# Second projections of two squared-ReLU MLPs: seven products of quarters in place of eight, sums kept on chip, and other buffer counts

## The chip, the cores and the metric

The kernel runs on one core of a Trainium2 chip. The metric is the time of one execution on the device in microseconds (us), the median of the runs that were made. Each run's profile also gives a span, which is the time from its first to its last recorded instruction.

## What is computed

Two transformer blocks follow each other on 512 tokens of width 1024, in float32. The first block has a hybrid mixer, a cross attention and a gated MLP. The second block has two layers, and each of them has a mixer (a sparse attention in the first, a gated linear attention in the second), a layer norm, an MLP and another layer norm. The change touches only the two MLPs of the second block. What one of them computes, cut from the reference:

```python
def sqrelu_mlp(x, w1, w2):
    return jnp.square(jax.nn.relu(x @ w1)) @ w2
...
        x = layer_norm(ALPHA * x + mix, ln1_g[i], ln1_b[i])
        x = layer_norm(ALPHA * x + sqrelu_mlp(x, mlp_w1[i], mlp_w2[i]), ln2_g[i], ln2_b[i])
```

Here x is 512 x 1024, w1 is 1024 x 4096 and w2 is 4096 x 1024. So the second projection multiplies a 512 x 4096 hidden matrix by w2 and adds the result to ALPHA times x.

## The kernel before, in words

**Precision.** Every float32 matrix is held as two parts, a rounded high part and the rest, the low part (class `Split`). One product of two such matrices is three matmuls in one PSUM group: high by high, high by low, low by high (`mm`). A weight piece of 128 x 512 is made into its parts by one ScalarE copy (high) and one VectorE subtraction (low), in `split`. In the profile the parts are the tiles wh and wl, and wr is the raw tile that the DMA fills.

**The MLP (`mlp`).** The 4096 hidden units are taken in eight rounds of 512. In a round, four calls of `proj_t` compute four hidden tiles of 128 hidden units by 512 tokens: 8 products of 128 x 128 by 128 x 512, so 24 matmuls each, with weights from `unit_t` (one raw tile of 512 KB, split in two halves). ScalarE takes the ReLU out of PSUM into the tile r, VectorE or GpSimd squares it (`either`), and ScalarE and VectorE split it into the pair hid. Then `proj_n` of the round before runs: four weight units (`unit_n`), and for each of 4 token tiles and 2 halves of the 1024 output columns a PSUM group of 4 x 3 = 12 matmuls of 512 columns. Each group is added into x by one VectorE instruction (round 0 multiplies x by ALPHA in the same instruction). The last round's projection is returned as steps and runs together with the layer norm that follows (`tail`, `ln_norm`), whose output is transposed for the next stage.

**Buffers.** Four pools matter. Raw tiles wr come from a pool of `N_RAW` = 3. Pages of 1056 float32 (`N_PAGE` = 33) hold the two parts of a weight unit (two pages), of a hidden pair (one page) and of the transposed input (eight pages). Half pages of 512 (`N_HALF` = 18) hold r and similar tiles. PSUM has eight banks.

**Order.** The program is first recorded (`Recorder`), and a planner (`Plan`) sets the order of every engine's instructions by a list schedule over its own prices. So first projections of one round and second projections of the one before can be interleaved. A load may start only when its raw tile is free and when the unit nine places ahead of it in the list `units` has been used for the last time (the quota, 9 in the MLPs). A tile may take a buffer ahead of older ones only within the limits of `rules`: two PSUM banks and two pages are kept back for older tiles, and at most ten older PSUM tiles may be passed over. Where the plan shows TensorE idle for over 1 us, `emit` fills the gap with matmuls of the identity (`warm`), which show in the profile as `ps<-ident` 128x512.

All calls are issued from one place, so every row of the profile has line L509. The tile names tell the operations apart.

Of the kernel before, what the change touches and what calls it, by code (L numbers as in the profile page):

```python
# [7 lines left out]
F32 = mybir.dt.float32  # L8
F32R = mybir.dt.float32r
I32 = mybir.dt.int32  # L10
BF16 = mybir.dt.bfloat16
AF = mybir.ActivationFunctionType
OP = mybir.AluOpType
# [3 lines left out]
P = 128  # L17
# [6 lines left out]
ALPHA = 4.0 ** 0.25  # L24
# [3 lines left out]


PAGE = 1056  # L30
N_PAGE = 33
N_HALF = 18
N_RAW = 3
ROUNDS = 8
BIAS = 0.0

# [8 lines left out]
def is_ap(x):  # L45
    return hasattr(x, "ap") and hasattr(x, "tensor") and hasattr(x, "offset")


def on_chip(x):
    return type(x.tensor).__name__ == "Tile"  # L50
# [19 lines left out]
def region(ap):  # L70

    per = 1
    for s in list(ap.tensor.shape)[1:]:
        per *= int(s)
    dims = [(int(s), int(n)) for s, n in ap.ap]
    p0, f0 = divmod(int(ap.offset), per)
    pn = dims[0][1] if dims[0][0] else 1
    mask = 1
    for s, n in sorted((s, n) for s, n in dims[1:] if s and n > 1):
        m = 0  # L80
        if s == 1 and mask == 1:
            m = (1 << n) - 1
        else:
            for k in range(n):
                m |= mask << (k * s)
        mask = m
    return ap.tensor.name, p0, p0 + pn, mask << f0
# [10 lines left out]
class Recorder:  # L98
# [10 lines left out]
    def add(self, forms, bias=0.0):  # L109

        if self.held is not None:
            self.held += forms[0]
            return
        o = Op()
        o.i = len(self.ops)
        o.reads, o.writes, o.keep = [], [], self.keep
        for eng, method, args, kw in forms[0]:
            outs = [kw["out"] if "out" in kw else args[0]]
            if kw.get("accum_out") is not None:
                outs.append(kw["accum_out"])  # L120
            ins = [x for x in (args if "out" in kw else args[1:]) if is_ap(x)]
            ins += [x for k, x in kw.items() if k not in ("out", "accum_out") and is_ap(x)]
            for x in outs + ins:
                if on_chip(x):
                    self.tiles[x.tensor.name] = x.tensor
            o.writes += [region(x) for x in outs if on_chip(x)]
            o.reads += [region(x) for x in ins if on_chip(x)]
        o.forms = [(f[0][0], f) + price(f) + (bias if f[0][0] == "vector" else 0.0, port(f)) for f in forms]
        self.ops.append(o)
        return o  # L130
# [57 lines left out]
def port(calls):  # L188

    for eng, m, args, kw in calls:  # L190
        if eng not in ("vector", "gpsimd") or m in ("memset", "iota", "dma_start"):
            continue
        out = kw["out"] if "out" in kw else args[0]
        ins = [x for x in list(args[1:]) + [x for k, x in kw.items() if k not in ("out", "accum_out")] if is_ap(x)]
        room = [x for x in ins if "PSUM" not in str(x.space) and width(x) > 1]
        if eng == "gpsimd" or len(room) > 1:
            return True
        if m in ("tensor_copy", "tensor_scalar") and room and "PSUM" not in str(out.space):
            return True
    return False  # L200


def price(calls):

    t = sum(price1(*c) for c in calls)
    eng = calls[0][0]
    return t, {"tensor": 0.22, "scalar": 0.16, "vector": 0.12, "gpsimd": 0.12, "sync": 0.9}[eng]
# [325 lines left out]
class Block:  # L533
    def __init__(self, ctx, tc, a, out):
# [4 lines left out]
        self.const = E(tc.tile_pool(name="const", bufs=1))  # L539
        self.wp = E(tc.tile_pool(name="wp", bufs=N_RAW))  # L540
        self.pgp = E(tc.tile_pool(name="pgp", bufs=N_PAGE))
        self.s2p = E(tc.tile_pool(name="s2p", bufs=N_HALF))
# [257 lines left out]
    def proj_n_steps(self, part, w, r0, alpha=None, us=None, fine=False):  # L800
# [4 lines left out]
        for i in range(NT):  # L805
            for h in self.HALVES:
# [9 lines left out]
                        nc.vector.scalar_tensor_tensor(xv, xv, alpha, ps, op0=OP.mult, op1=OP.add)  # L816
                yield

    def setup(self):
        nc, a, cp = self.nc, self.a, self.const  # L820
        for i in range(NT):
            for c in self.HALVES:
                nc.sync.dma_start(self.x[:, i, c], a["x"][0, i * P:(i + 1) * P, c])
        self.identr = cp.tile([P, P], F32R, name="ident")
        self.ident = self.identr.bitcast(F32)
        t = self.s2()
        nc.gpsimd.memset(t[:, 0:P], 0.0)
        nc.gpsimd.affine_select(t[:, 0:P], t[:, 0:P], pattern=[[-1, P]], compare_op=OP.not_equal, fill=1.0, base=0,
                                channel_multiplier=1)
        nc.vector.tensor_copy(self.identr, t[:, 0:P])  # L830

        self.mnegr = cp.tile([P, P], F32R, name="mnegr")
        nc.gpsimd.memset(t[:, P:2 * P], 0.0)
        nc.gpsimd.affine_select(t[:, P:2 * P], t[:, P:2 * P], pattern=[[-1, P]], compare_op=OP.is_ge, fill=NEG, base=0,
                                channel_multiplier=1)
        nc.vector.tensor_copy(self.mnegr, t[:, P:2 * P])
        self.cols = {}
# [503 lines left out]
    def mlp(self, l, xT):  # L1341
        nc, a = self.nc, self.a
        w1, w2 = a["mlp_w1_2"][l], a["mlp_w2_2"][l]
        self.rules(9)
        self.early = 5
        prev = None
        for c in range(8):
            hid = []
            for j in range(4):
                ps = self.proj_t(self.unit_t(w1, (c * 4 + j) * P), xT)  # L1350
                r = self.s2("r")
                nc.scalar.activation(r, ps, AF.Relu)
                self.either("tensor_mul", r, r, r)
                h = self.pair("hid")
                self.split(h.hi, h.lo, r)
                hid.append(h)
            if prev:
                self.proj_n(prev, w2, (c - 1) * 512, None if c > 1 else ALPHA)
            prev = hid
        return self.proj_n_steps(prev, w2, 7 * 512, fine=l == 1)  # L1360

    def nsa(self, xT):
# [532 lines left out]
```

## Time and profile before

| what | value |
|---|---|
| median of 3 runs | 1964.53 us (1963.47 to 1973.55) |
| profiled execution, time | 1964.42 us |
| profiled execution, span | 1962.6 us |
| TensorE matmul busy | 1930.5 us (98%) |
| TensorE weight load busy | 1645.3 us (84%) |
| VectorE busy | 1214.9 us (62%) |
| ScalarE busy | 824.2 us (42%) |
| GpSimd busy | 78.5 us (4%) |
| mean granted TensorE clock | 0.994 |

PE is TensorE's matmuls, PEld its weight loads, DVE VectorE, ACT ScalarE, POOL GpSimd, SPq the queue that issues the DMAs. Matmuls are pipelined and overlap in the records, so the time that one takes in a stream is the distance between two starts, not its recorded length. The same holds for VectorE and ScalarE instructions that follow each other without a wait. The MLPs take roughly 1010 to 1376 us and 1590 to 1955 us of the span, each with parts of its neighbours at the ends.

### The profile page before, as it was taken

To read this page: it belongs to the slowest core of one execution; us is meant where nothing else is said; L and a number is where in the kernel's file an instruction comes from. 1 tells how busy PE (TensorE), PEld (TensorE's weight loads), DVE (VectorE), ACT (ScalarE), POOL (GpSimd) and SP (SyncE) were. 2 spreads that over 40 slices of the span, in tenths; PEclk is the share of its full clock that TensorE was granted. 3 is DMA by queue.
4 is the path that set the end of the run, shared out by engine and by line. 5 is a ranking of instruction groups with operands and counts; after the bars stand their busy time and mean duration, and the time that the engine had idled before them with its cause. 6 is when DMAs were issued, how large, how long until landed. Compare 5 with 4: busy or idle time off the path is not lost.

```text
span 1962.6 us, 26913 instructions
## 1 busy us (share of the span) xinstructions
PE 1930.5 (98%) x10348; PEld 1645.3 (84%) x10348; DVE 1214.9 (62%) x2690; ACT 824.2 (42%) x1673; POOL 78.5 (4%) x123
## 2 busy tenths in 40 slices
PE   9999999999999999999999999999999999999998
PEld 8888889798888878988788888778998988888776
DVE  5999665565434457688884345347686775344356
ACT  5476534344322333576534233233575434223330
POOL 0021000000000000012200000000000000000001
PEclk9999999999999999999999999999999999999999
DMA  6222423323222433510332233243223322233241
GB/s 172 80 69 65 155 87 103 97 65 118 65 76 75 118 108 83 110 32 22 99 106 76 75 108 97 75 127 104 76 76 97 98 76 91 67 98 105 70 150 43
DMA packets 215466, 177.38 MB, mean 90 GB/s; under 512 B 25174, under 2 KB 194202, under 8 KB 215338
## 3 DMA queue, kind: packets, MB, share of 16 engines
q1 hardware_dynamic: 215338, 175.66, 30.6%
q8 instruction: 81, 1.33, 0.3%
q14 instruction: 47, 0.39, 0.1%
HBM read 173.54 MB, written 2.10 MB: 89 GB/s over the span
## 4 chain that ended last, share of the span: by engine, by line
PE 86%; DVE 9%; ACT 3%; DMA 2%; issue 1%; SPq 0%; POOL 0%; DVEq 0%; ACTq 0%
PE ps L509 86%; DVE wl L509 2%; DVE sm L509 1%; DVE gcv L509 1%; ACT wh L509 1%; ACT p L509 1%; DMA wr<-in_mlp_w_dram 1%; DVE xtl L509 0%; DVE x L509 0%; DVE pt L509 0%; DMA wr<-in_w_up_dram 0%; ACT xth L509 0%; DMA g<-in_norm_mix_g_dram 0%; DMA wr<-in_w_down_dram 0%; DMA wr<-in_a_w_out_dram 0%
## 5 line engine op out<-in xcount | busy, mean ns | idle before, releaser
L509 ACT ACTIVATE wh<-wr 128x512 fp32r<-128x512 f32 x625 | 357.1, 623 | 423.5 <-PE ps L509 271.5
L509 DVE TENSOR_TENSOR wl<-wr,wh 128x512 fp32r<-128x512 f32 x625 | 406.2, 686 | 205.6 <-PE ps L509 96.8
L509 PE MATMUL ps<-xth,wh 128*128 128x512 f32 (+1 forms) x1464 | 516.9, 353 | 0.4 <-ACT hg L509 0.4
L509 PE MATMUL ps<-xtl,wh 128*128 128x512 f32 (+1 forms) x1464 | 514.4, 351 | 1.4 <-DVE xtl L509 1.4
L509 PE MATMUL ps<-xth,wl 128*128 128x512 f32 (+1 forms) x1464 | 513.4, 351 | 0.0
L509 PE MATMUL ps<-wh,hid 128*128 128x512 f32 (+1 forms) x1392 | 436.4, 391 | 1.8 <-ACT wh L509 1.7
L509 PEld LDWEIGHTS ps<-wh,hid 128*128 128x128 f32 x1392 | 260.3, 188 | 61.6 <-ACT wh L509 3.3
L509 PEld LDWEIGHTS ps<-xtl,wh 128*128 128x128 f32 x1464 | 276.2, 189 | 41.4 <-DVE xtl L509 2.6
L509 PEld LDWEIGHTS ps<-xth,wh 128*128 128x128 f32 x1464 | 276.4, 189 | 40.2 <-ACT xth L509 0.8
L509 PEld LDWEIGHTS ps<-xth,wl 128*128 128x128 f32 x1464 | 275.7, 188 | 39.9 <-DVE wl L509 0.2
L509 PE MATMUL ps<-wl,hid 128*128 128x512 f32 (+1 forms) x696 | 272.4, 391 | 1.6 <-DVE wl L509 1.5
L509 DVE TENSOR_TENSOR x<-x,ps 128x512 f32<-128x512 f32 (+1 forms) x210 | 141.1, 678 | 162.8 <-PE ps L509 162.2
L509 PEld LDWEIGHTS ps<-wl,hid 128*128 128x128 f32 x696 | 130.8, 188 | 34.2 <-DVE wl L509 4.8
L509 DVE TENSOR_TENSOR r<-r 128x512 f32<-128x512 f32 x62 | 42.8, 691 | 99.8 <-ACT r L509 99.7
L509 PE MATMUL ps<-wl,xth 128*128 128x256 f32 (+2 forms) x320 | 94.4, 295 | 3.4 <-DVE wl L509 3.4
L509 PE MATMUL ps<-wh,xth 128*128 128x256 f32 (+2 forms) x320 | 94.7, 296 | 0.0
L509 PE MATMUL ps<-wh,xtl 128*128 128x256 f32 (+2 forms) x320 | 93.9, 293 | 0.0
L509 ACT ACTIVATE r<-ps 128x512 f32<-128x512 f32 x64 | 38.0, 593 | 114.9 <-PE ps L509 114.9
L509 DVE SCALAR_TENSOR_TENSOR cv<-ps,cols,cv 128x511 f32<-128x511 f32 (+2 forms) x56 | 41.8, 746 | 39.1 <-ACT cv L509 38.5
L509 PEld LDWEIGHTS ps<-wl,xth 128*128 128x128 f32 x320 | 60.4, 189 | 5.6 <-DVE wl L509 4.2
L509 PE MATMUL ps<-wh,o 128*128 128x512 f32 x192 | 62.3, 394 | 0.0
L509 PEld LDWEIGHTS ps<-wh,xth 128*128 128x128 f32 x320 | 60.3, 189 | 1.4
(352 smaller groups left out, 2438.9 us busy)
## 6 DMA issues: line engine op xcount, KB each, us to landing
wr<-in_mlp_w_dram SPq DMA_DIRECT2D x128, 512.0 KB, 4.2
wr<-in_w_up_dram SPq DMA_DIRECT2D x44, 512.0 KB, 3.9
wr<-in_c_w_in_dram SPq DMA_DIRECT2D x24, 512.0 KB, 3.8
wr<-in_w_down_dram SPq DMA_DIRECT2D x22, 512.0 KB, 3.6
wr<-in_w_in_dram SPq DMA_DIRECT2D x16, 512.0 KB, 4.3
wr<-in_w_xkv_dram SPq DMA_DIRECT2D x16, 512.0 KB, 3.8
wr<-in_w_out_dram SPq DMA_DIRECT2D x8, 512.0 KB, 4.5
wr<-in_w_xq_dram SPq DMA_DIRECT2D x8, 512.0 KB
```

Source lines behind the costliest of these rows:

```text
L509: getattr(getattr(self.rec.nc, eng), method)(*args, **kw)
```

## The change

The second projection of rounds 0 to 6 of each MLP is done by the Winograd form of Strassen's scheme. The hidden tiles are taken two at a time (K of 256), and each pair is cut into quarters of 128 hidden units by 256 tokens. The 256 rows of w2 that belong to it are cut into quarters of 128 rows by 512 columns. Seven products of such quarters take the place of eight.

- `quad` makes the left sides from a pair of squared tiles: four additions or subtractions of 256 columns, and splits of one quarter of 256 columns and three tiles of 512 columns. It fills three pages and one half page, where the two hidden pairs took two pages.
- `wquad` loads two raw tiles (the 256 rows of w2) and makes the seven right sides when they are asked for. Four of the seven need a subtraction of 512 columns first, written over a quarter of the raw tile. Each right side is split into a page of its own. So both raw tiles stay taken until the last product (`p4`) has been made.
- `proj_s` takes the place of `proj_n` in rounds 0 to 6: for each product and each of two token tiles a PSUM group of 2 x 3 = 6 matmuls of 512 columns. Three of the products are added into x, four are kept as sums in half pages over all seven rounds (eight tiles; the first round copies them out with ScalarE).
- `join` adds the eight sums into x, with 16 VectorE instructions, once per MLP, ahead of the last round's projection, which stays as it was.
- The square of the ReLU goes to ScalarE or VectorE, no longer to VectorE or GpSimd.
- The pools change for the whole program: `N_RAW` 3 to 5, `N_PAGE` 33 to 31.

The diff, cut to what the text speaks of:

```diff
-N_PAGE = 33
+N_PAGE = 31
 N_HALF = 18
-N_RAW = 3
+N_RAW = 5
...
+    def quad(self, ra, rb):
+        x11, x21, x12, x22 = ra[:, 0:256], ra[:, 256:512], rb[:, 0:256], rb[:, 256:512]
+        u, v = self.s2("sum"), self.s2("sum")
+        s1, s2, s3, s4 = u[:, 0:256], u[:, 256:512], v[:, 0:256], v[:, 256:512]
+        nc.vector.tensor_add(s1, x21, x22)
+        nc.vector.tensor_sub(s2, s1, x11)
+        nc.vector.tensor_sub(s3, x11, x21)
+        nc.vector.tensor_sub(s4, x12, s2)
+        h = self.s2("q1", F32R)
+        q1 = Split(h[:, 0:256], h[:, 256:512])
+        self.split(q1.hi, q1.lo, x11)
+        ps = []
+        for src in (rb, u, v):
+            q = self.pair("qd")
+            self.split(q.hi, q.lo, src)
+            ps += [q[:, 0:256], q[:, 256:512]]
...
+    def wquad(self, w, r0):
+        for j in range(2):
+            t = self.wp.tile([P, 1024], F32, tag="wr", name=self.uid("wr"))
+            firsts.append(len(nc.ops))
+            nc.sync.dma_start(t, w[r0 + j * P:r0 + (j + 1) * P, :])
+            raw.append(t)
+        w11, w12, w21, w22 = (t[:, c] for t in raw for c in self.HALVES)
...
+            src = {"p2": w21, "p3": w22, "p7": w12}.get(k, w11)
+            if k == "p5":
+                sub(w11, w12, w11)
+            elif k == "p6":
+                sub(w11, w22, w11)
+            elif k == "p7":
+                sub(w12, w22, w12)
+            elif k == "p4":
+                sub(w11, w21, w11)
+            u = self.pair("wq")
+            self.split(u.hi, u.lo, src, weights=True)
+            if k in ("p3", "p4"):
+                nc.units.append(([firsts[k == "p3"]], u.hi.tensor.name, self.quota))
...
+    def proj_s(self, quads, w, r0, sums, alpha=None):
+        make = [self.wquad(w, r0 + 2 * k * P) for k in range(len(quads))]
+        to = dict(p2=(0, lo), p3=(0, hi), p4=(2, lo))
+        for p in ("p1", "p2", "p5", "p3", "p6", "p7", "p4"):
+            us = [m(p) for m in make]
+            for t in range(2):
+                ps = self.ps()
+                for k, (q, u) in enumerate(zip(quads, us)):
+                    self.mm(ps, q[p][:, t * P:(t + 1) * P], u, k == 0, k == len(quads) - 1)
+                if p not in to:
+                    new = (p, t) not in sums
+                    if new:
+                        sums[p, t] = self.s2("acc")
+                        nc.scalar.activation(sums[p, t], ps, AF.Copy)
+                    else:
+                        nc.vector.tensor_add(sums[p, t], sums[p, t], ps)
+                    continue
+                xv = self.x[:, to[p][0] + t, to[p][1]]
...
+    def join(self, sums, alpha=None):
+        for t in range(2):
+            p1, p5, p6, p7 = (sums[p, t] for p in ("p1", "p5", "p6", "p7"))
+            x11, x12, x21, x22 = (self.x[:, i + t, c] for i in (0, 2) for c in (lo, hi))
+            add(x11, x11, p1)
+            add(p6, p6, p1)
+            add(x12, x12, p6)
+            add(x12, x12, p5)
+            add(p7, p7, p6)
+            add(x21, x21, p7)
+            add(p7, p7, p5)
...
-                self.either("tensor_mul", r, r, r)
-                h = self.pair("hid")
-                self.split(h.hi, h.lo, r)
-                hid.append(h)
+                nc.add([[("scalar", "activation", (r, r, AF.Square), {})], [("vector", "tensor_mul", (r, r, r), {})]])
+                if c < 7:
+                    rs.append(r)
+                    if len(rs) == 2:
+                        hid.append(self.quad(*rs))
+                        rs = []
...
             if prev:
-                self.proj_n(prev, w2, (c - 1) * 512, None if c > 1 else ALPHA)
+                self.proj_s(prev, w2, (c - 1) * 512, sums, None if c > 1 else ALPHA)
             prev = hid
+        self.join(sums, ALPHA)
         return self.proj_n_steps(prev, w2, 7 * 512, fine=l == 1)
```

## Rows read from the trace of the kernel before

**Rows 1.** The page, part 1: busy time, share and instructions of each engine.

```profile
PE 1930.5 (98%) x10348; PEld 1645.3 (84%) x10348; DVE 1214.9 (62%) x2690; ACT 824.2 (42%) x1673; POOL 78.5 (4%) x123
```

**Rows 2.** Busy time by stretch, steady part of each MLP; columns as the first line says.

```profile
core 0: us, PE busy (x) PEld busy (x) DVE busy (x) ACT busy (x) POOL busy (x), PEclk, DMA share, GB/s
1060.00:1320.00 260.00, 259.28 (x1117) 209.26 (x1116) 111.17 (x174) 75.89 (x135) 4.70 (x11) 1.00 0.30 89
...
1640.00:1880.00 240.00, 238.94 (x1031) 192.75 (x1029) 100.71 (x158) 66.74 (x120) 1.29 (x1) 1.00 0.29 87
```

**Rows 3.** Timeline of PE in the first MLP: start, length, what.

```profile
1197.80 0.40 PE L509 MATMUL ps<-xth,wh 128*128 128x512 f32 x1
...
1203.38 0.40 PE L509 MATMUL ps<-wh,hid 128*128 128x512 f32 x1
```

**Rows 4.** Timeline of DVE: runs of instructions without a wait, and what follows them.

```profile
1109.08 3.70 DVE L509 TENSOR_TENSOR wl<-wr,wh 128x512 fp32r<-128x512 f32 x6
1112.70 0.67 DVE L509 TENSOR_TENSOR x<-x,ps 128x512 f32<-128x512 f32 x1
...
1374.27 4.05 DVE L509 TENSOR_TENSOR xtl<-ps,xth 128x256 fp32r<-128x256 f32 x12
1378.25 0.68 DVE L509 BATCH_NORM_STATS2 sm<-x 128x6 f32<-128x512 f32 x1
```

**Rows 5.** Timeline of ACT: four copies without a wait.

```profile
1108.85 2.20 ACT L509 ACTIVATE wh<-wr 128x512 fp32r<-128x512 f32 x4 [21.67 <-PE ps L509]
```

**Rows 6.** Groups by form in 1060 to 1320 us: busy, mean ns, idle before and its releaser.

```profile
L509 DVE TENSOR_TENSOR wl<-wr,wh 128x512 fp32r<-128x512 f32 x84 | 53.8, 686 | 40.4 <-ACT wh L509 22.9 <-PE ps L509 17.4
L509 ACT ACTIVATE wh<-wr 128x512 fp32r<-128x512 f32 x84 | 48.4, 622 | 120.0 <-PE ps L509 74.4 <-DMA wr<-in_mlp_w_dram 43.2 <-issue 2.4
L509 ACT ACTIVATE r<-ps 128x512 f32<-128x512 f32 x24 | 14.2, 593 | 49.8 <-PE ps L509 49.8
```

**Rows 7.** Groups by form of the whole span: 256-column low parts and their copies.

```profile
L509 DVE TENSOR_TENSOR xtl<-ps,xth 128x256 fp32r<-128x256 f32 x112 | 38.9, 414 | 7.4 <-ACT xth L509 7.1
L509 ACT ACTIVATE xth<-ps 128x256 fp32r<-128x256 f32 x112 | 33.1, 410 | 21.0 <-PE ps L509 20.7
```

**Rows 8.** Busy time by stretch where DVE is loaded; columns as in the group of steady stretches.

```profile
50.00:100.00 50.00, 49.92 (x237) 40.81 (x236) 48.68 (x77) 25.69 (x37) 0.00 (x0) 1.00 0.29 84
...
840.00:960.00 120.00, 114.24 (x721) 100.40 (x720) 103.05 (x306) 82.31 (x233) 28.48 (x44) 0.96 0.11 34
...
1340.00:1380.00 40.00, 40.00 (x206) 33.79 (x205) 37.19 (x90) 14.29 (x30) 0.00 (x0) 1.00 0.33 92
...
1420.00:1460.00 40.00, 40.00 (x333) 39.51 (x333) 34.15 (x93) 27.33 (x60) 0.00 (x0) 1.00 0.20 58
...
1540.00:1600.00 60.00, 59.53 (x336) 51.34 (x335) 52.91 (x131) 27.11 (x60) 2.97 (x2) 1.00 0.29 79
```

**Rows 9.** Groups by form in 50 to 100 us: matmuls that fill planned gaps.

```profile
L509 PE MATMUL ps<-ident 128*128 128x512 f32 x76 | 17.7, 391 | 0.0
```

**Rows 10.** Busy time by stretch ahead of the two MLPs' ends.

```profile
1320.00:1340.00 20.00, 20.00 (x88) 16.20 (x87) 12.95 (x22) 6.94 (x13) 0.00 (x0) 1.00 0.37 119
...
1907.00:1928.00 21.00, 21.00 (x93) 17.08 (x92) 6.41 (x11) 0.00 (x0) 0.00 (x0) 1.00 0.00 1
```

**Rows 11.** Loads of MLP weights: the issue's duration and the time to landing.

```profile
L509 SPq DMA_DIRECT2D wr<-in_mlp_w_dram x128: 327/354/1646, 962.4 to 1900.1; - x128
...
DMA to landing us min/median/max: 3.4/4.2/5.6
```

**Rows 12.** Waits of the DMA queue in 1035 to 1340 us: total, times, longest.

```profile
SPq L509 <- DVE wl L509: 259.0, 52, 27.8
```

**Rows 13.** Waits of PE and its weight loads, whole span: total, times, longest.

```profile
PEld ps L509 <- DVE wl L509: 10.4, 17, 1.5
...
PE ps L509 <- DVE wl L509: 5.1, 10, 1.3
```

More of the change, by code (lines that the diff above doesn't have):

```diff
@@ L817, in proj_n_steps @@
                 yield
+    def quad(self, ra, rb):
+        nc = self.nc
+        x11, x21, x12, x22 = ra[:, 0:256], ra[:, 256:512], rb[:, 0:256], rb[:, 256:512]
[13 more added lines that the diff above has]
+            ps += [q[:, 0:256], q[:, 256:512]]
+        x12, x22, s1, s2, s3, s4 = ps
+        return dict(p1=q1, p2=x12, p3=s4, p4=x22, p5=s1, p6=s2, p7=s3)
@@ new lines, in wquad, with make @@
+    def wquad(self, w, r0):
+        nc = self.nc
+        raw, firsts = [], []
+        for j in range(2):
[4 more added lines that the diff above has]
+        w11, w12, w21, w22 = (t[:, c] for t in raw for c in self.HALVES)
+        sub = nc.vector.tensor_sub
+        def make(k):
+            src = {"p2": w21, "p3": w22, "p7": w12}.get(k, w11)
[11 more added lines that the diff above has]
+                nc.units.append(([firsts[k == "p3"]], u.hi.tensor.name, self.quota))
+            return u
+        return make
@@ new lines, in proj_s @@
+    def proj_s(self, quads, w, r0, sums, alpha=None):
+        nc = self.nc
+        make = [self.wquad(w, r0 + 2 * k * P) for k in range(len(quads))]
+        lo, hi = self.HALVES
+        to = dict(p2=(0, lo), p3=(0, hi), p4=(2, lo))
[14 more added lines that the diff above has]
+                xv = self.x[:, to[p][0] + t, to[p][1]]
+                if alpha is not None:
+                    nc.vector.scalar_tensor_tensor(xv, xv, alpha, ps, op0=OP.mult, op1=OP.add)
+                else:
+                    nc.vector.tensor_add(xv, xv, ps)
@@ new lines, in join @@
+    def join(self, sums, alpha=None):
+        nc = self.nc
+        add = nc.vector.tensor_add
+        lo, hi = self.HALVES
+        for t in range(2):
[8 more added lines that the diff above has]
+            add(p7, p7, p5)
+            if alpha is None:
+                add(x22, x22, p7)
+            else:
+                nc.vector.scalar_tensor_tensor(x22, x22, alpha, p7, op0=OP.mult, op1=OP.add)
@@ L1346, in mlp @@
         prev = None
+        sums = {}
         for c in range(8):
-            hid = []
+            hid, rs = [], []
             for j in range(4):
@@ L1352, in mlp @@
                 nc.scalar.activation(r, ps, AF.Relu)
-                self.either("tensor_mul", r, r, r)
-                h = self.pair("hid")
-                self.split(h.hi, h.lo, r)
-                hid.append(h)
+                nc.add([[("scalar", "activation", (r, r, AF.Square), {})], [("vector", "tensor_mul", (r, r, r), {})]])
[4 more added lines that the diff above has]
+                        rs = []
+                else:
+                    h = self.pair("hid")
+                    self.split(h.hi, h.lo, r)
+                    hid.append(h)
             if prev:
-                self.proj_n(prev, w2, (c - 1) * 512, None if c > 1 else ALPHA)
+                self.proj_s(prev, w2, (c - 1) * 512, sums, None if c > 1 else ALPHA)
             prev = hid
+        self.join(sums, ALPHA)
         return self.proj_n_steps(prev, w2, 7 * 512, fine=l == 1)
```

## The prediction

> **What bounds the kernel now.** I read the engines' shares first [rows 1]: TensorE is busy for 98% of the span, VectorE for 62%, so the matmul stream sets the time. The shares are means over stages, so next come the steady stretches of the two MLPs [rows 2]. There TensorE is idle for 0.72 of 260 us and 1.06 of 240 us, while VectorE is 43% and 42% busy and ScalarE 29% and 28%. In the MLPs nothing but TensorE counts, and a matmul that is taken away shortens the kernel by its pace, as long as the other engines keep up. The pace comes from the timeline, not from the recorded length of 0.39 us: 24 matmuls start between 1197.80 and 1203.38 us, so 5.58/24 = 0.2325 us each [rows 3]. VectorE's pace is read in the same way: six 512-column subtractions from 1109.08 to 1112.70 us give 0.603 us each, and twelve of 256 columns give 3.98/12 = 0.332 us [rows 4]. ScalarE: four copies in 2.20 us, of which the last takes 0.62, so 0.53 us each [rows 5, 6].
>
> **What it removes.** A round's second projection has 8 groups of 12 matmuls, 96 in all. After the change it has 7 products x 2 token tiles x 6 matmuls = 84. Twelve fewer per round, 7 rounds, 2 MLPs: 168 matmuls x 0.2325 = 39.1 us, all of it on the path that sets the end. A round goes from 192 x 0.2325 = 44.6 us to 180 x 0.2325 = 41.9 us. The profiled execution took 1964.42 us, 1.8 us over its span and 0.1 us under the median of the runs, so I add nothing between the two. The floor is 1964.4 - 39.1 = 1925.3 us.
>
> **What it adds to VectorE.** Before, a round has 16 low parts of weights, 4 squares, 4 low parts of hidden tiles and 8 evictions: 32 x 0.603 = 19.3 us of 44.6, 43%, which is what the steady stretches show [rows 2]. After, a full round (rounds 1 to 6, those that make quarters and also run a second projection) has 8 low parts of first weights, 14 of second weights, 8 subtractions for the right sides, 6 low parts of quarters and 14 evictions, which is 50 x 0.603 = 30.2 us, and 8 additions and 2 low parts of 256 columns, 10 x 0.332 = 3.3 us. That is 33.5 us of 41.9, or 80%. The squares I count to ScalarE, which has 22 copies of weights (11.7 us), 4 ReLUs (2.4), 4 squares (2.1), 6 copies of quarters (3.2) and 2 of 256 columns (0.8 [rows 7]): 20 us, 48%. ScalarE is no limit. VectorE stays under TensorE, but it goes from a helper with half its time free to one with 8.4 us to spare per round.
>
> One rule of the skill speaks against this part. The rows show that VectorE instructions with no wait start closer together than their length: 0.603 us apart where one takes 0.686 [rows 4, 6]. The Trainium skill, VectorE: DVE Perf Modes, "The DRAIN you can't avoid", says that the next instruction does not start until the pipe of the one before is empty; the same page excepts instructions that are not held. By full lengths the load would be 50 x 0.686 + 10 x 0.414 = 38.4 us of 41.9, 92% [rows 6, 7]; that is the first rival below, with a low chance, since the six subtractions here were plainly not held.
>
> **What the load costs TensorE.** No row shows this mix, so I bound the idle time from stretches in which VectorE is 85% to 97% busy [rows 8]. In three of them (1340 to 1380, 1420 to 1460, 1540 to 1600 us; projections with their weight splits and norms) TensorE is idle for 0, 0 and 0.47 us of 140 us together, 0.3%. In 840 to 960 us (softmax chains) it loses 5.8 of 120 us, 4.8%. In 50 to 100 us VectorE is at 97% and the plan had to put in 76 filling matmuls, 76 x 0.2325 = 17.7 us, over a third of the stretch [rows 9]; I leave that stretch out of the sum, because a saturated engine is another case than one at 80%, but it shows what happens if my load is wrong. The twelve full rounds take 12 x 41.9 = 502 us, so the bounds are 1.5 and 24 us. I take 1.5%, 7.5 us: nearer to the first three, which are weight splits under projections too, yet above them, because one product has only 12 matmuls (2.8 us) and needs 2 low parts, 1.1 subtractions on average and 2 evictions, some 3.1 us of VectorE, so TensorE must mix first projections in between.
>
> **The join** is 16 VectorE instructions of 512 columns per MLP, 16 x 0.603 = 9.6 us, and all of the last round's evictions queue behind those on the same parts of x. In the second MLP VectorE is idle for 14.6 of 21 us just before the last norm [rows 10], so it is covered, as long as the last seven products end early enough. In the first MLP it is free for 7 of 20 us before 1340 us [rows 10] and nearly full for the 40 us after [rows 8]. The bounds are 0 and 9.6 us; I take 3, since 7 of 9.6 find room. If that cover were gone, the whole 9.6 us would show as a late transposed input for the next stage.
>
> **Buffers.** The loads are the same in number and bytes. Five raw tiles for three: the DMA queue now waits for raw tiles to be split for 259 us in the first MLP [rows 12], yet TensorE hardly notices. The new code keeps four raw tiles until the last product is made, so the first projections have one left while a second projection runs. One tile turns over in a landing (4.2 us [rows 11]), then the copy and the subtraction of two halves, some 2 us more; four in a round are 25 us of 41.9, so it suffices. Of the 31 pages the transposed input holds 8 and the quarters of two rounds 12, which leaves 11 for weights where 17 were left; a product needs two and a first-projection unit two, so about four to five steps can be ready ahead, and with two pages kept back, three to four. Other stages get two pages fewer and two raw tiles more. All that earlier weights could give back to TensorE there is 15.5 us of waits, some of it counted twice [rows 13]; I put the effect at zero, between -5 and +6 us.
>
> **Sum.** 1925.3 + 7.5 + 3 = 1935.8, say 1936 us, 1.5% less than before.
>
> **Rivals.**
> First, VectorE is the bound in effect: 92% by full lengths, or 80% with hand-overs to ScalarE (copy, then subtraction) that leave holes in it. TensorE then loses the 4.8% of the worst comparable stretch, 24 us, and the join finds no room, 9.6 us a time for the first MLP at least: 1925.3 + 24 + 9.6 = 1959 us, no difference that can be told. For it speaks that a product asks for 3.1 us of VectorE in 2.8 us of TensorE; against it that quarters and weights are made a round ahead.
>
> Second, slower: the raw tiles. The quota counts nine units back, and a round has eight (four first weights, four raw tiles of w2), so the load that is last in a round waits for the use of the last product (p4) of the round before. Then comes the landing, 4.2 us, the copy, 0.7 us, and the subtraction, 0.7 us, before that pair's first product can run: a gap of 5.6 us per round, which only first projections can fill. A ready unit of first weights is 24 x 0.2325 = 5.6 us of cover, so one is just enough. If none is ready, because one raw tile and few pages were left for it, twelve gaps cost 67 us: 1925.3 + 67 + 3 = 1995 us. It decides from (39.1 - 3)/12 = 3.0 us per round. Against it: the quota lets the first weights be loaded a round ahead, and at the time one needs only two of 11 pages.
>
> Third, it does less than it says: two pages fewer disturb stages that the change doesn't touch, by more than my +6. The price at the upper end is a few us, 1945 us, and the sign doesn't turn.
>
> **How the numbers follow.** About 0.5% is what a measurement of this kernel can tell from no change, so faster is under 1954.7 us and slower above 1974.4. My forecast with its own bounds (1926 to 1952) has 0.64, the first rival (1945 to 1968) 0.18, the second 0.13, the third 0.05. From the first rival a third counts as faster; the second is mostly slower. So faster is 0.64 + 0.06 + 0.05 = 0.75, same 0.12 + 0.01 = 0.13, slower 0.12. The range runs from 1925 (the floor; raw tiles that help elsewhere against some idle time) to 1962 us, which leaves out the second rival and the top of the first.
>
> **What would show it.** Right: 168 fewer matmuls at the same 0.2325 us, VectorE at about 80% in the steady stretches, ScalarE near 48%, TensorE idle by 1 to 2% there, no ACT_TABLE_LOAD in the MLPs for the square, and the join in stretches where VectorE was free. First rival: VectorE above 90% and matmuls that wait for wl or wq of VectorE again and again. Second rival: one gap of several us per round, ended by a copy that itself waited for a DMA, or filling matmuls in the MLPs, of which there are none now. The forecast fails most easily if the order of products and first projections can't be mixed as freely as I assume, for that is where the 1.5% comes from.

## The result, and the profile after

The kernel after takes 1935.74 us (median of 4 runs, 1933.6 to 1937.69) against 1964.66 us before; the ratio is 0.9843, 95% interval 0.9812 to 0.9874. The profiled execution has a span of 1933.3 us, 29.3 us less than before. The forecast was 1936 us. The total came out as predicted, but two of the terms in it did not, and they nearly cancel.

The page, part 1, of the kernel after (compare [rows 1]: TensorE's share as before, VectorE from 62% to 73%, ScalarE from 42% to 49%, and 170 matmul records fewer: 168 that the change takes away, and of the filling matmuls 12 fewer ahead of the first MLP and 10 more in the linear attention):

```profile
PE 1886.2 (98%) x10178; PEld 1608.7 (83%) x10178; DVE 1418.2 (73%) x3107; ACT 944.0 (49%) x1883; POOL 83.2 (4%) x123
```

Busy time by stretch, kernel after. The first three lines are the first MLP, the linear attention and the second MLP. A stage begins where the last part of its transposed input is written, and the second MLP is taken up to the last matmul. The next three lines are full rounds, the last two the end of the kernel (compare [rows 2, 8, 10]):

```profile
core 0: us, PE busy (x) PEld busy (x) DVE busy (x) ACT busy (x) POOL busy (x), PEclk, DMA share, GB/s
1016.90:1361.83 344.93, 340.10 (x1582) 279.27 (x1582) 284.74 (x534) 172.63 (x314) 7.94 (x13) 1.00 0.31 94
1361.83:1587.14 225.31, 222.24 (x1592) 206.09 (x1592) 161.73 (x377) 124.44 (x232) 4.35 (x4) 1.00 0.29 89
1587.14:1910.05 322.91, 322.91 (x1475) 265.32 (x1474) 256.21 (x449) 154.39 (x278) 0.00 (x0) 1.00 0.29 89
1050.00:1150.00 100.00, 100.00 (x433) 81.11 (x432) 79.44 (x139) 50.97 (x91) 0.00 (x0) 1.00 0.32 95
1150.00:1250.00 100.00, 100.00 (x434) 81.31 (x433) 79.74 (x141) 50.23 (x89) 0.42 (x1) 1.00 0.36 114
1740.00:1840.00 100.00, 100.00 (x432) 80.75 (x431) 83.90 (x149) 50.80 (x91) 0.00 (x0) 1.00 0.34 103
1900.00:1910.00 10.00, 10.00 (x67) 9.04 (x65) 10.00 (x19) 0.00 (x0) 0.00 (x0) 1.00 0.01 2
1910.00:1920.00 10.00, 0.05 (x1) 0.00 (x0) 9.83 (x46) 4.34 (x6) 4.39 (x4) 0.70 0.01 2
```

In these stretches of full rounds VectorE is at 79% to 84%, ScalarE at 50% to 51%, and TensorE has no idle time at all. In the first MLP TensorE is idle for 344.93 - 340.10 = 4.8 us. Of that, 3.4 us lie in the step to the linear attention, from 1342 us on, and 1.4 us in a full round, inside a row of matmuls of products:

```profile
1261.66 8.31 PE L509 MATMUL ps<-wq,qd 128*128 128x512 f32 x35
1270.83 0.51 PE L509 MATMUL ps<-wq,qd 128*128 128x512 f32 x1 [0.86 <-ACT wq L509]
1271.91 1.42 PE L509 MATMUL ps<-wq,qd 128*128 128x512 f32 x5 [0.58 <-DVE wq L509]
```

Here wq is a right side and qd a left side. VectorE works without a break from 1253.9 us until past this gap, and the ScalarE copy that TensorE waits for had itself waited for VectorE's subtraction. The second MLP has no idle time up to its last matmul.

The same stages of the kernel before, where the last matmul ends at 1954.07 us (its start at 1953.79 and 0.28):

```profile
1029.76:1387.34 357.58, 356.86 (x1659) 293.63 (x1657) 184.37 (x328) 116.03 (x213) 4.70 (x11) 1.00 0.31 92
1387.34:1609.74 222.40, 219.59 (x1590) 206.10 (x1589) 160.34 (x375) 119.06 (x229) 3.28 (x3) 1.00 0.31 91
1609.74:1954.07 344.33, 341.95 (x1557) 279.78 (x1555) 166.17 (x283) 102.12 (x180) 10.61 (x8) 1.00 0.28 87
```

So the 29.3 us are made up like this:

| stretch | before | after | change |
|---|---|---|---|
| up to the first MLP's input | 1029.8 | 1016.9 | -12.9 |
| first MLP | 357.6 | 344.9 | -12.7 |
| linear attention | 222.4 | 225.3 | +2.9 |
| second MLP, to the last matmul | 344.3 | 322.9 | -21.4 |
| behind the last matmul | 8.5 | 23.3 | +14.7 |

What happens behind the last matmul is on VectorE's and GpSimd's timelines. In them acc is a kept sum, sm holds the norm's small statistics and g its gain. VectorE of the kernel after, the last 32 us:

```profile
1901.73 0.68 DVE L509 TENSOR_TENSOR acc<-acc,ps 128x512 f32<-128x512 f32 x1
1903.53 0.68 DVE L509 TENSOR_TENSOR acc<-acc,ps 128x512 f32<-128x512 f32 x1
...
1911.80 0.69 DVE L509 SCALAR_TENSOR_TENSOR x<-x,acc 128x512 f32<-128x512 f32 x1
...
1913.26 1.56 DVE L509 SCALAR_TENSOR_TENSOR sm<-sm,sm 128x1 f32<-128x1 f32 x16
...
1917.38 6.30 DVE L509 SCALAR_TENSOR_TENSOR sm<-sm,sm 128x1 f32<-128x1 f32 x6
1923.60 2.07 DVE L509 SCALAR_TENSOR_TENSOR x<-x,sm,g 128x512 f32<-128x512 f32 x3
1925.59 3.70 DVE L509 TENSOR_TENSOR x<-x,g 128x512 f32<-128x512 f32 x6
```

GpSimd of the kernel after, the same stretch:

```profile
1915.61 7.87 POOL L509 TENSOR_TENSOR x<-x,g 128x512 f32<-128x512 f32 x6 [348.67 <-ACT x L509]
```

And VectorE of the kernel before at the same step, the small instructions of the last token tile's norm:

```profile
1956.88 1.30 DVE L509 SCALAR_TENSOR_TENSOR sm<-sm,sm 128x1 f32<-128x1 f32 x6
```

The last kept sums leave PSUM at 1901.7 and 1903.5 us, only some 7 us before the last matmul. They come that late because the plan put the last 27 matmuls of the seven products behind three quarters of the last round's projection, whose 512-column matmuls (`ps<-wh,hid`, `ps<-wl,hid`) end before them:

```profile
1897.94 6.41 PE L509 MATMUL ps<-wq,qd 128*128 128x512 f32 x27
```

The join ends at 1912.5 us, and the small steps of the norms of the first three token tiles, which used to run under the last projection, come with it or after it, from 1910.76 us on. Their six multiplications by the gain then run on GpSimd from 1915.61 to 1923.48 us. Under them the six small instructions of the last tile's norm take 6.30 us, where the same six took 1.30 us before. The Trainium skill, GPSIMD Engine Reference, "1. Specifications", says that GpSimd shares its SBUF interfaces with VectorE and that instructions with two SBUF inputs contend with it; the row agrees, with about 1.2 us for an instruction that takes 0.2 us alone (five of the six; the last one starts when GpSimd is done).

### The profile page after: what moved, and what is told of

Same layout as the page of the kernel before. It is cut to its first block, busy times and chain, and to the rows that moved or that the text cites. A ratio compares the mean times of both kernels' runs of the same rounds, so it can differ in the third digit from the quotient of the medians.

```text
span 1933.3 us, 27259 instructions
## 1 busy us (share of the span) xinstructions
PE 1886.2 (98%) x10178; PEld 1608.7 (83%) x10178; DVE 1418.2 (73%) x3107; ACT 944.0 (49%) x1883; POOL 83.2 (4%) x123
## 3 DMA queue, kind: packets, MB, share of 16 engines
q8 instruction: 80, 1.31, 0.3%
## 4 chain that ended last, share of the span: by engine, by line
PE 78%; DVE 15%; ACT 3%; issue 1%; DMA 1%; SPq 1%; DVEq 0%; ACTq 0%
PE ps L509 78%; DVE sm L509 3%; DVE x L509 3%; DVE wl L509 2%; DVE gcv L509 2%; ACT L509 1%; SPq L509 1%; DVE pt L509 1%; DVE acc L509 1%; ACT wh L509 1%; DVE p L509 0%; DVE cv L509 0%; DVE xtl L509 0%; DVE gs L509 0%; ACT xth L509 0%
## 5 line engine op out<-in xcount | busy, mean ns | idle before, releaser
L509 DVE TENSOR_TENSOR wl<-wr,wh 128x512 fp32r<-128x512 f32 x513 | 333.2, 683 | 126.6 <-PE ps L509 78.5
L509 ACT ACTIVATE wh<-wr 128x512 fp32r<-128x512 f32 x513 | 290.3, 622 | 187.9 <-PE ps L509 131.0
L509 PE MATMUL ps<-wq,qd 128*128 128x512 f32 x1008 | 244.6, 394 | 1.4 <-ACT wq L509 0.9
L509 PEld LDWEIGHTS ps<-wq,qd 128*128 128x128 f32 x1008 | 189.4, 188 | 46.2 <-ACT wq L509 1.3
L509 DVE TENSOR_TENSOR x<-x,ps 128x512 f32<-128x512 f32 (+1 forms) x186 | 124.8, 678 | 77.4 <-PE ps L509 77.2
L509 ACT ACTIVATE wq<-wr 128x512 fp32r<-128x512 f32 x196 | 117.7, 625 | 79.6 <-DVE wr L509 36.9
L509 PE MATMUL ps<-wh,hid 128*128 128x512 f32 (+1 forms) x496 | 154.3, 386 | 0.2 <-ACT wh L509 0.2
L509 DVE TENSOR_TENSOR wq<-wr,wq 128x512 fp32r<-128x512 f32 x196 | 130.9, 688 | 14.0 <-ACT wq L509 13.5
L509 PEld LDWEIGHTS ps<-wh,hid 128*128 128x128 f32 x496 | 92.2, 188 | 20.8 <-ACT wh L509 0.7
L509 PE MATMUL ps<-wl,hid 128*128 128x512 f32 (+1 forms) x248 | 95.9, 387 | 0.2 <-DVE wl L509 0.2
```

Source lines behind the costliest of these rows:

```text
L509: getattr(getattr(self.rec.nc, eng), method)(*args, **kw)
```

## Experiments

Theory A, formed from the two traces: TensorE gets nearly the whole 39.1 us, some of the rest comes from the buffers, and the late join costs 14.7 us at the end. The rivals were those of the prediction (VectorE as the bound in effect; the reload gap of the raw tiles) and, for the end of the kernel, a tail that comes from something other than the place of the join. Each comparison with the kernel before has its own runs beside it.

**Buffers alone.** The kernel before with

```diff
-N_PAGE = 33
+N_PAGE = 31
-N_RAW = 3
+N_RAW = 5
```

> The kernel before with 5 raw tiles and 31 pages, nothing else. Theory A (TensorE gets the whole 39.1 us, about 5 us come from the buffers in stages that the change does not touch, and 14.7 us are lost behind the last matmul): 1960 us, 1956 to 1962. Theory B (the stage marks of the two traces: input of the first MLP 12.9 us earlier, linear attention 2.9 us longer, so 10 us from the buffers, and the MLPs lose 20 of 39.1): 1954 us. Theory C (as predicted, buffers give nothing): 1964 us.

Measured: 1964.17 us (1961.17 to 1965.15), ratio 0.9994 (0.9984 to 1.0003). The sum is zero, as the prediction had it, and theories A and B both fall on this point. But the parts are not zero. Busy time by stage, buffers alone:

```profile
1018.23:1373.46 355.23, 355.07 (x1659) 293.68 (x1658) 184.20 (x327) 116.03 (x213) 5.70 (x12) 1.00 0.30 93
1373.46:1605.54 232.08, 226.38 (x1604) 209.63 (x1603) 161.72 (x372) 124.88 (x233) 7.09 (x6) 0.99 0.29 87
1605.54:1947.34 341.80, 340.51 (x1553) 279.76 (x1551) 159.51 (x278) 101.58 (x180) 5.89 (x5) 1.00 0.26 81
```

The first MLP's input is there 11.5 us earlier than before, as in the kernel after. Then the linear attention takes 9.7 us longer and the stretch behind the last matmul 4.9 us longer (1960.7 - 1947.34 = 13.4). In the kernel after, with the same buffers, the linear attention takes only 225.3 us. The two runs that follow show what goes with it: 231.2 us with seven products in the first MLP alone, 225.8 us with seven products in the second MLP alone. So the shorter stage goes with the second MLP's seven products; by which step of the plan is not shown.

**One MLP at a time.** Both with the buffers of the kernel after; QUADS is the number of rounds by seven products in each MLP, and the join follows the last of them:

```diff
-                if c < 7:
+                if c < QUADS[l]:
                     rs.append(r)
...
-            if prev:
+            if prev and c <= QUADS[l]:
                 self.proj_s(prev, w2, (c - 1) * 512, sums, None if c > 1 else ALPHA)
+                if c == QUADS[l]:
+                    self.join(sums, ALPHA)
+            elif prev:
+                self.proj_n(prev, w2, (c - 1) * 512, None if c > 1 else ALPHA)
             prev = hid
-        self.join(sums, ALPHA)
```

QUADS = (7, 0):

> Seven products only in the first MLP; the second MLP has the eight products, still with the square on ScalarE or VectorE; 5 raw tiles, 31 pages. Measured from the run with the buffers alone: theory A 19.5 us less, and some 4 us lost at its join, so 15 to 16 us less. Theory B, 12.6 us less.

QUADS = (0, 7):

> Seven products only in the second MLP, 5 raw tiles, 31 pages. Measured from the run with the buffers alone: theory A (the join just ahead of the last norm costs 14.7 us behind the last matmul) 19.5 - 14.7 = about 5 us less. Rival (the loss lies in the rounds, evenly in both MLPs, and the tail is an accident of one schedule): about 14 us less, as in the first.

Measured: 1945.26 us (0.9904, 0.9889 to 0.9919) with the first alone, and 1948.91 us (0.9923, 0.9908 to 0.9938) with the second alone, so 18.9 and 15.3 us less than the buffers alone. The first gives more than theory A expected. The second misses theory A's 5 us and fits the rival's 14; but theory A's figure was reckoned from a short tail, and the run with the buffers alone has a tail of 13.4 us of its own. The trace of the second alone shows the pile-up again: the last matmul ends at 1924.6 us, 23.1 us before the end, and six small instructions take 6.31 us. The two gains add up to 34.2 us, 5.7 us more than both together gave, so single stages cannot be priced to better than some 6 us in this way. Much of it is the tail: the run with the first alone ends 9.2 us behind its last matmul, some 4 us less than the buffers alone.

**The join one round earlier.** QUADS = (7, 6): in the second MLP, round 6 goes by eight products.

> The kernel after, but in the second MLP only rounds 0 to 5 use seven products and the join follows round 5, one round earlier; round 6 uses the eight products. That is 12 matmuls, 2.8 us, more on TensorE. Theory A (the join piles up on the last norm): the stretch behind the last matmul goes from 23 us back to 8 to 10 us, so 1935.7 + 2.8 - 14 = 1925 us, 1922 to 1929. Rival (the tail comes from the VectorE load of the rounds, not from the place of the join): 1938 us.

Measured: 1925.15 us (1924.5 to 1928.12), ratio 0.9801 (0.9785 to 0.9818), 10.6 us less than the kernel after with 12 matmuls more. Timeline of VectorE, then the last matmul:

```profile
1884.18 0.69 DVE L510 TENSOR_TENSOR acc<-acc,ps 128x512 f32<-128x512 f32 x1
...
1920.67 1.30 DVE L510 SCALAR_TENSOR_TENSOR sm<-sm,sm 128x1 f32<-128x1 f32 x6
```

```profile
1915.82 0.28 PE L510 MATMUL ps<-wh,hid 128*128 128x256 f32 x1
```

The last kept sum now leaves PSUM 32 us before the last matmul, the small instructions take 1.30 us again, and the stretch behind the last matmul is 1926.4 - 1916.1 = 10.3 us. The tail falls by 13.0 us, where theory A expected 14. The edit also makes round 6 plain, so this run alone does not separate the place of the join from a lighter last stretch. The two runs with more work for VectorE, below, do: with the join in its late place and VectorE loaded to 92% and up to 99% in the rounds, the stretch behind the last matmul is 22.1 us (1938.5 - 1916.4) and 21.6 us (1952.7 - 1931.1), no longer than with 80%. So the tail comes from the late join and not from the load of the rounds. Whether the same join would be covered if the plan put the last products ahead of the last projection was not tried.

**GpSimd's part in the tail.** The kernel after with

```diff
-                    nc.gpsimd.tensor_mul(xc, xc, gt[:, c])
+                    self.either("tensor_mul", xc, xc, gt[:, c])
```

> The kernel after, with the last norm's multiplication by its gain allowed on VectorE or GpSimd where it was fixed to GpSimd. Of the 23.3 us behind the last matmul, 6.3 us were six tiny VectorE instructions of 1.20 us each, while GpSimd worked off six multiplications. Theory A1 (those instructions are slow because GpSimd works at the same time): they go back to about 0.2 us, 5 us less, and VectorE takes on some of the multiplications, 0.6 us each, so 1931 to 1934 us, still a tail of about 20 us. Theory A2 (the pile-up of the norms behind the join alone makes the tail, GpSimd is no matter): 1936 us.

Measured: 1932.44 us (0.9833, 0.9818 to 0.9848). The interval overlaps that of the kernel after, so the gain in time is not shown by the runs alone, but the trace shows the mechanism. VectorE takes the multiplications, GpSimd does nothing at the end, and a small instruction takes 0.2 us between them:

```profile
1919.02 0.69 DVE L509 TENSOR_TENSOR x<-x,g 128x512 f32<-128x512 f32 x1
1919.62 0.21 DVE L509 SCALAR_TENSOR_TENSOR sm<-sm,sm 128x1 f32<-128x1 f32 x1
```

The last matmul ends at 1911.7 us, 19.5 us before the end, in place of 23.3. So by these two traces GpSimd's contention, less what the six multiplications cost on VectorE, made 3.8 of the 14.7 us; that the pile-up made the rest is what is left over.

**More work for VectorE.** The low part of a weight is computed twice, at first for the first weights (8 instructions more per round), then for the second weights (14 more):

```diff
             if weights:
                 nc.scalar.activation(hi, src, AF.Copy)
-                nc.vector.tensor_sub(lo, src, hi.bitcast(F32))
+                for _ in range(1 + self.dup):
+                    nc.vector.tensor_sub(lo, src, hi.bitcast(F32))
```

> The kernel after, with the low parts of the first weights computed twice in rounds 1 to 6 of both MLPs: 8 VectorE instructions more per round, so 33.5 + 4.8 = 38.3 us of 41.9, 92%, the load that the first rival assumed. Theory A (TensorE runs free as long as VectorE's work fits into the round): within 5 us of the kernel after, 1936 to 1941 us. Rival 1 of the prediction (at 92% TensorE loses 4.8% of 502 us): 1960 us.

> The kernel after, with the low parts of the second weights computed twice in all rounds but the first that uses them: 14 VectorE instructions more per round, so 33.5 + 8.4 = 41.9 us of 41.9, 100%. Theory A: VectorE becomes the bound, and each of the twelve rounds lengthens by what does not fit, 2 to 4 us with the usual small gaps, so 1960 to 1985 us. Rival (hand-overs leave holes already at lower loads): well over 1985 us.

Measured: 1937.05 us (0.9853, 0.9837 to 0.987) with 8 more, which is 1.3 us over the kernel after, and 1955.59 us (0.9956, 0.9941 to 0.9971) with 14 more, 19.9 us over it. Busy time by stretch, 8 more:

```profile
1150.00:1250.00 100.00, 99.56 (x431) 80.31 (x430) 93.39 (x165) 51.46 (x90) 0.00 (x0) 1.00 0.38 116
1740.00:1840.00 100.00, 99.45 (x427) 79.53 (x426) 91.68 (x162) 48.39 (x88) 0.00 (x0) 1.00 0.32 100
```

14 more, and what TensorE waited for in that run:

```profile
1150.00:1250.00 100.00, 99.54 (x430) 80.41 (x430) 97.49 (x173) 49.75 (x89) 0.00 (x0) 1.00 0.34 106
1640.00:1740.00 100.00, 95.21 (x403) 76.25 (x402) 87.37 (x153) 45.42 (x83) 0.00 (x0) 0.98 0.27 80
1740.00:1840.00 100.00, 99.92 (x432) 80.59 (x431) 99.15 (x176) 51.88 (x93) 0.00 (x0) 1.00 0.36 112
```

```profile
PE ps L509 <- DVE wq L509: 10.8, 7, 4.0
```

At 92% to 93% TensorE is idle for about 0.5 us of 100. In the second of these windows four filling matmuls, 0.9 us, hide a gap of the plan besides:

```profile
1759.82 1.09 PE L509 MATMUL ps<-ident 128*128 128x512 f32 x4
```

Over the twelve rounds the idle and the filled time are 3.4 us, 0.7%, where the kernel after has 1.4 us. So the first rival falls: the load that it assumed costs some 2 us and not 24. With 14 more VectorE sets the pace where products stand in a row. TensorE waits for second weights for up to 4.0 us at a time (at 1724.98 us, behind 31 matmuls of products, with VectorE at work without a break), even in the stretch where VectorE's mean is only 87%; eleven filling matmuls stand in that stretch too. Theory A's lower end was 1960 us, so this load cost a little less than expected.

**Four raw tiles.** The kernel after with

```diff
-N_RAW = 5
+N_RAW = 4
```

> The kernel after with four raw tiles in place of five, so that while a pair of quarters is in use no raw tile is left for the first weights. Rival 2 of the prediction (the reload gap that only a ready unit of first weights covers): the gap of 5.6 us opens in twelve rounds, 67 us at most, 1975 to 2003 us. Theory A (pages hold enough ready units, so raw tiles are not what TensorE waits for): 1936 to 1945 us.

Measured: 1949.45 us (0.9922, 0.9907 to 0.9937), 13.7 us over the kernel after. Neither fits. The gap of the second rival does not open in every round. TensorE looks full in the rounds, but seven matmuls in each MLP only fill a gap of the plan; the kernel after has none of these in its MLPs:

```profile
1229.34 1.77 PE L509 MATMUL ps<-ident 128*128 128x512 f32 x7
1766.93 1.79 PE L509 MATMUL ps<-ident 128*128 128x512 f32 x7
```

That is 14 x 0.2325 = 3.3 us, with 2.6 us of idle time, in place of 67 us. At both places VectorE works without a break, and the last copy of second weights before them had waited for VectorE and not for a DMA. At the first of them the next first weights were still on their way (their copy starts at 1231.5 us and had waited for the DMA), so there the missing raw tile plays a part. By stretch:

```profile
1050.00:1150.00 100.00, 99.72 (x431) 80.67 (x431) 75.98 (x133) 50.21 (x91) 0.00 (x0) 1.00 0.28 84
1150.00:1250.00 100.00, 99.94 (x430) 80.59 (x430) 79.07 (x140) 52.03 (x93) 0.00 (x0) 1.00 0.40 121
1740.00:1840.00 100.00, 100.00 (x435) 81.18 (x434) 79.81 (x140) 49.62 (x88) 0.00 (x0) 1.00 0.33 99
1345.00:1372.00 27.00, 23.12 (x143) 19.89 (x142) 24.97 (x62) 12.54 (x29) 4.05 (x5) 0.87 0.13 39
```

Part of the loss is in the step from the first MLP to the linear attention, the last line, where TensorE is idle for 3.9 of 27 us, 16 more matmuls only fill planned gaps, and the granted clock averages 0.87. By stage the first MLP with this step takes 7.0 us more than in the kernel after, the second MLP 3.6 and the linear attention 2.7. That a gap of 5.6 us in every round is not the cause is shown; what in the plan made the rest is not.

**The first MLP's join one round earlier too.** QUADS = (6, 6).

> As the run with six rounds in the second MLP, and the first MLP also joins after round 5 and does round 6 with eight products: 12 matmuls, 2.8 us, more. If the late join costs the step from the first MLP to the linear attention 3 us, as predicted, this is even with 1925 us; if it costs 6 us (3.4 us of idle TensorE and ten filling matmuls, 2.3 us, were seen there), 1922 us; if it costs nothing, 1928 us.

Measured: 1920.81 us (0.9772, 0.9754 to 0.9791). Against the run with (7, 6), whose first MLP takes 344.94 us with 4.8 us idle, just as in the kernel after, the first MLP is 2.6 us shorter, and TensorE has no idle time left. Of its 21 more matmul records 12 are round 6 by eight products, and seven fill a gap of the plan in a round (1.6 us):

```profile
1018.33:1360.65 342.32, 342.32 (x1603) 283.13 (x1603) 269.26 (x498) 170.76 (x311) 5.18 (x11) 1.00 0.32 98
```

```profile
1228.22 1.78 PE L510 MATMUL ps<-ident 128*128 128x512 f32 x7
```

So the late join cost 5.4 us there by the trace (2.6 + 2.8), and 7.0 us if the filled gap is counted as a loss of this plan, which agrees with the medians (4.3 + 2.8).

**The last norm not pinned, with the early join.** QUADS = (7, 6) with the edit of the GpSimd experiment.

> The run with six rounds in the second MLP, and the last norm's multiplications free to go to VectorE or GpSimd. There the norms of the first three token tiles no longer pile up, and the six tiny instructions take 1.30 us together in place of 6.30. So theory A expects nothing from it: 1925 us, within 2 us. If GpSimd's work alone had been the cost, it would again be 3 us less, 1922 us.

Measured: 1922.98 us (0.9786, 0.9769 to 0.9802), between the two expectations. The interval overlaps that of the run without the edit, and in the two traces the difference is already there at the first MLP's input (1014.7 against 1019.8 us), before anything that was edited. The stretch behind the last matmul is 9.5 us against 10.3. So the edit itself is worth about nothing there.

**The gated MLP of the first block.** QUADS = (7, 6), and in `ffn` the second projection of rounds 0 to 3 by `quad` and `proj_s`, joined ahead of round 4's projection:

```diff
+                if c0 < 4 * 4:
+                    rs.append(cv)
+                    if len(rs) == 2:
+                        hid.append(self.quad(*rs))
+                        rs = []
+                    continue
...
-            if prev:
+            if prev and c0 <= 4 * 4:
+                self.proj_s(prev[1], w_dn, prev[0] * P, sums)
+                if c0 == 4 * 4:
+                    self.join(sums)
+            elif prev:
                 self.proj_n(prev[1], w_dn, prev[0] * P)
```

> The run with six rounds in the second MLP, and the second projection of the first block's gated MLP also by seven products in its rounds 0 to 3, joined a round before the end. 4 x 12 = 48 matmuls fewer, 11.2 us. VectorE there: 16 low parts of up weights, 14 + 8 for the right sides, 12 instructions of the gate's convolution and product, quarters and 14 evictions, some 47 us of the 64 us of a round, 73%. Theory A (below 92% the products cost TensorE nothing): 1914 us, 1912 to 1918. Rival (the scheme pays only in a loop as plain as these MLPs'): 1925 us or more.

Measured: 1916.02 us (0.9752, 0.9735 to 0.977), 9.1 us under the run with (7, 6), of 11.2 taken away (the plan alone had moved the first MLP's input by 5 us in the run before, so the 9.1 us are no better known than that). The steady stretch of that stage:

```profile
440.00:720.00 280.00, 280.00 (x1213) 227.57 (x1212) 194.98 (x327) 117.75 (x203) 0.59 (x3) 1.00 0.31 93
```

TensorE has no idle time there, with VectorE at 70%.

**All together.** QUADS = (6, 6), the last norm's multiplications not pinned, four rounds of the gated MLP.

> All three steps together: six rounds in each MLP, the last norm's multiplications free, four rounds of the gated MLP. If the steps add up, 1925.2 - 4.3 (six and six) - 2.2 (not pinned) - 9.1 (gated MLP) = 1909.6 us; between 1906 and 1914 us, since every change of one stage moves the planned order of the others by a few us.

Measured: 1910.46 us (1907.89 to 1913.14), ratio 0.9725 (0.9699 to 0.975). This beats both kernels: 25 us less than the kernel after.

## Why the prediction was right

**What it removes.** Right in count and pace. In the second MLP 82 matmul records are missing of the 84 (a few are lost in the records), and the stage up to the last matmul is 21.4 us shorter, where 84 x 0.2325 is 19.5 and the kernel before was idle there for 2.4 us more. In the first MLP 12.7 of 19.5 us are gained. Of the rest 4.1 us are new idle time (4.8 against 0.7), and its records fall by 77 in place of 84, 1.6 us; some 1 us stays open.

**What it adds to VectorE.** Right: 80% forecast, 79% to 84% measured; ScalarE 48% forecast, 50% to 51% measured; and no ACT_TABLE_LOAD falls into either MLP. By full instruction lengths VectorE would have been at 92%. The Trainium skill's rule in VectorE: DVE Perf Modes, "The DRAIN you can't avoid", would have given that; the trace does not agree for these instructions, which start every 0.60 us at a length of 0.69 us, and the exception that the page makes fits.

**What the load costs TensorE.** Mis-sized. 1.5% of twelve rounds, 7.5 us, was forecast; the rounds show 1.4 us, 0.3%, all at one place. The reason given for the 1.5%, that TensorE must mix first projections in between, is not borne out: the longest rows are 78 matmuls of products without one, and of the two that long one has the 1.4 us (1253.1 to 1273.2 us) and the other no idle time (1167.8 to 1185.8 us). By the prediction's own 3.1 and 2.8 us seven products in a row leave VectorE only some 2 us behind, an estimate that sides made ahead can cover. The other step that failed is the choice of rows: the bound of 24 us came from 840 to 960 us, and there TensorE's waits in the kernel before are mostly for ScalarE and GpSimd, 3.6 us against 1.5 us for VectorE:

```profile
PE ps L509 <- ACT p L509: 2.6, 4, 0.9
PE ps L509 <- POOL p L509: 1.0, 1, 1.0
PE ps L509 <- DVE pt L509: 1.0, 2, 0.5
PE ps L509 <- DVE cs L509: 0.5, 1, 0.5
```

The two runs with repeated subtractions give the curve itself: 0.3% at 80%, 0.7% at 92%, and 20 us on the whole kernel near 100%. The first rival is ruled out, and only near 100% does VectorE decide.

**The join.** This term failed in the second MLP. I put it at zero because VectorE was idle for 14.6 of 21 us ahead of the last norm [rows 10], "as long as the last seven products end early enough". They did not: the sums came out of PSUM up to 7 us before the last matmul, and 14.7 us were lost behind it, 13.0 of which came back with the earlier join. I had looked for room on an engine and not for the time at which the join's inputs are there and what queues behind it. In the first MLP the term was 3 us, and 5 to 7 were measured.

**Buffers.** Zero was forecast, and the buffers alone gave 0.2 us (1964.17 against 1964.35 us). But in the kernel after the stages outside the MLPs are 10 us shorter (-12.9 and +2.9), beyond my bounds of -5 and +6. This gain and the 14.7 us of the join nearly cancel; so the 1936 us hold partly by luck. By the terms: the MLPs with their tail gained 12.7 + 21.4 - 14.7 = 19.4 us, where 28.6 were forecast, and 10 us came from where zero was forecast.

**The rivals.** The second rival's reload gap did not open; with four raw tiles the rounds lost 5.9 us, filled time included, of the 67 us that it asked for, and the other part of the 13.7 us came in another way. The third is there in parts but not in the sum: with the buffers alone the linear attention takes 9.7 us more, and the first MLP's input comes 11.5 us earlier.

## What to carry to other kernels

Where one engine's stream bounds a kernel and its helpers have half their time free, see how far work may be moved to them by loading the helper on purpose; here VectorE could be filled to 92%, with work prepared ahead, for 0.7% of TensorE's time. Count the matmuls that only fill gaps of the plan as idle time, for they hide it in the busy share. A reduction that is kept back to the end may belong one step earlier than it could stand: here the last round by the plain way cost 2.8 us and gave back 13 (10.6 net). And a forecast should be held against the stages one by one, for a right total can hide two wrong terms.

## What the runs showed of the hardware that I had not expected

- Tiny VectorE instructions (128 x 1, two inputs in SBUF) took about 1.2 us each while GpSimd multiplied 128 x 512 tiles (1.31 us each), against 0.2 us with GpSimd idle. The kernel before has it too: at 1944.24 us two of them took 1.23 us together, under two GpSimd multiplications. The price falls on a chain of dependent small steps, so it is far larger than GpSimd's few per cent of the span suggest.
- With VectorE 92% to 93% busy in two stretches of 100 us, TensorE was idle for about 0.5%, and lost 0.7% of the twelve rounds with the filled gaps.
- A change of pool sizes alone moved single stages by -11.5 to +9.7 us, with a sum near zero. The plan is made anew for each kernel, so this belongs to the planner and not to the chip.
